# Spreading the softmax reciprocals of each pair's first head by a transpose instead of a product with the identity

## The chip, the cores and the metric

The kernel runs on one core of one Trainium2 chip. A core has five engines that run side by side, each through its own list of instructions: TensorE (PE, matrix products; its weight loads are shown apart as PEld), VectorE (DVE), ScalarE (ACT), GpSimd (POOL) and SyncE (SP), which issues DMA transfers. Products read SBUF and write PSUM, a memory of 128 partitions in eight banks of 512 4-byte words each. The engines meet through semaphores. The metric is the device time of one execution in microseconds (us).

## The reference

One transformer layer for 128 context tokens and 512 latent tokens, with a model width of 1024. The change touches the attention alone: 16 query heads of 64 channels, 4 key and value heads (4 query heads share one).

```python
def block_attention(q, k, v):
    ...
    def one_block(qblk):
        s = jnp.einsum('bqkgd,btkd->bkgqt', qblk, k).astype(jnp.float32) * scale
        p = jax.nn.softmax(s, axis=-1).astype(v.dtype)
        return jnp.einsum('bkgqt,btkd->bqkgd', p, v)
```

Context queries see the 128 context keys. Latent queries see 128 cached context keys and 512 latent keys, 640 in all. Around it stand a projection of the normalised input, a gated short convolution, output projections, and a feed-forward part with a convolution.

## The kernel before, in words

The 640 tokens are five tiles of 128 rows: tile 0 is the context, tiles 1 to 4 are latent. The kernel first normalises the input and makes keys and values, then runs the attention, then everything else (projections, convolution, feed-forward), which is one long stream of products.

The attention runs from about 70 us to 226 us. For each of the four key and value heads g (loop over `NKV`) there are nine steps: one for the context tile, which takes four query heads in two pairs, and two for each latent tile, each of which takes one pair of query heads. That makes 36 steps, 4 of the context and 32 latent. Each step n has this course:

- `score` (L1063 to L1076, products at L1073): queries times keys. The contraction is over 64 channels only, so the two heads of a pair use two row halves of PE's array (`tile_position=(64 * h, 0)`, 64*128 in the profile).
- the maximum over each row (DVE, L1120 or L1085), the exponential with its row sum (ACT, L1128 or L1092), and the split of the result into two 16-bit halves (ACT L1134 or L1099, DVE or POOL L1139, L1141 or L1101).
- `inv` (DVE, L1147 or L1095): the reciprocals of the row sums, one column of 128 values for each head, in `marks` from column 8 on.
- a transposing DMA (SP, L1145 or L1103) that turns the probabilities, so that keys lie in partitions.
- `pv` (L1157 to L1172), on PE. First it spreads the reciprocals (L1162): for each head, the column of 128 reciprocals is read 64 times over (`broadcast_to((128, 64))`) as the stationary operand, and the 4-byte identity matrix is the moving one. The product is a 64 x 128 block, each row of which holds the 128 reciprocals: head 0 of a pair in partitions 0 to 63, head 1 in partitions 64 to 127, in columns 256 to 511 of the bank that the step's result goes to. Then it multiplies values by probabilities (L1170): 30 products of 16-bit operands for a latent step, 12 for a context step, alternating between the heads. The heads use two column halves of the array (`tile_position=(0, 64 * h)`, 128*64 in the profile).
- after the second pair: ACT copies the spread reciprocals to SBUF (`spread`, L1182), DVE multiplies the result by them (`whole`, L1186), and ACT and DVE write the result as two halves (L1189, L1192).

Between these stand the query projections (L709, whole array, 128*128), the transposes of the queries (L1034, 4-byte, whole array), the copies after them, and two products for gates (L1212, L1223, by the helper at L709).

All these pieces are recorded as `work` items with their dependencies and the buffers they need. The order in which they are issued is written out by hand in the string `PLAN` (L50 to L91), which `follow` (L722) walks through: each entry names an item, the engine that does it, and the buffers it takes. The transfers and POOL's work keep that order, too. PE, DVE and ACT run what is issued to them in this order.

A 4-byte product (type float32, not the rounded float32r of L709 and L1073) is executed as two passes, each with its own weight load, and each pass is one record of the profile. A transpose on PE is a product with the identity as moving operand and the flag `is_transpose` set; on 4-byte data it is one pass.

Of the kernel before, what the change touches and what calls it, by code (L numbers as in the profile page):

```python
# [112 lines left out]
def trunk_layer(ctx, tc, x_prompt, x_sample, cache_k, cache_v, c, c_ctx, w_ada, b_ada, g_pre1, g_post1, g_pre2,  # L113
# [600 lines left out]
    def work(name, eng, do, after=(), rooms=()):  # L714
        works.append(Work(name, eng, do, list(after), list(rooms)))
        return works[-1]
# [30 lines left out]
    with tc.tile_pool(name="att", bufs=1) as at:  # L747
# [45 lines left out]
        def at_bank(room, n=512):  # L793
            return bank_of(room.at[0][1])[:, 0:n]
# [4 lines left out]
        def slot(xs, room):  # L799
            return xs[room.at[0][1]]  # L800
# [99 lines left out]
        for t in range(NT):  # L900
# [30 lines left out]
            h = work(f"k{t} hi", "ACT", k_hi, [tk], [pk])  # L931
# [121 lines left out]
        for n, (g, t, pi) in enumerate(steps):  # L1053
# [103 lines left out]
            def pv(g=g, t=t, pi=pi, pvr=pvr, trs=trs, vc_=vc_, mk=mk):  # L1157
                p = at_bank(pvr)
                for i in range(2) if t == 0 else (pi,):
                    for h in range(2):  # L1160
                        c = 8 + 2 * i + h if t == 0 else 8 + h
                        PE.matmul(p[64 * h:64 * h + 64, 256 + 128 * i:384 + 128 * i], mk[:, c:c + 1].broadcast_to((128, 64)), ident,  # L1162
                                  start=True, stop=True, tile_position=(0, 64 * h), skip_group_check=True)
                ks = ((0, 5),) if t == 0 else tuple((k, k) for k in range(5))
                for i in range(2) if t == 0 else (pi,):
                    for k, s in ks:
                        for m, (w, part) in enumerate(((0, 0), (0, 1), (1, 0))):
                            for h in range(2):
                                src = slot(PT, trs[0])[:, 4 * part + 2 * i + h, :] if t == 0 else slot(PT, trs[h])[:, 5 * part + k, :]
                                PE.matmul(p[64 * h:64 * h + 64, i * 128:i * 128 + 128], VH[:, w, s, vc_], src, start=k == 0 and m == 0,  # L1170
                                          stop=k == ks[-1][0] and m == 2, tile_position=(0, 64 * h), skip_group_check=True)
            pvs.append(work(f"pv{n}", "PE", pv, [x[0] for x in pts[n]] + invs + v_ready, [pvr] + trs))  # L1172
            if pi in (None, 1):
                u = vcol[:, 2 * g + (t > 0):2 * g + (t > 0) + 1]
# [1350 lines left out]
```

## Time and profile before

| | us |
|---|---|
| median of 3 runs | 1074.85 (1074.67 to 1075.89) |
| the profiled execution | 1074.79 |
| its span, first to last instruction | 1073.0 |
| PE busy | 1056.8 (98%), 8216 records |
| weight loads busy | 995.4 (93%) |
| DVE busy | 899.9 (84%) |
| ACT busy | 598.4 (56%) |
| POOL busy | 133.1 (12%) |
| L1162, the changed line | 160 records, 16.0 us busy |
| L1170, the products behind it | 1008 records, 34.3 us busy |

A record of PE is a pass; passes overlap at their ends, since the next one enters the array before the last one has left it, so busy times add up to more than the path. The views give, for a group of instructions, line, engine, operation, the tile written and the tiles read, the part of the array used (rows*columns), shape, type and count. The chain of work that ended last starts from the last instruction and goes back, at each step, to what released it. In the chain in order of time, a row has its start, its length, the engine, tile and line, and a count when rows are merged. A list of waits has the waiting engine, tile and line, whom it waited for, the total in us, how many times, and the longest.

### The profile page before, as it was taken

To read this page: it belongs to the slowest core of one execution; us is meant where nothing else is said; L and a number is where in the kernel's file an instruction comes from. 1 tells how busy PE (TensorE), PEld (TensorE's weight loads), DVE (VectorE), ACT (ScalarE), POOL (GpSimd) and SP (SyncE) were. 2 spreads that over 40 slices of the span, in tenths; PEclk is the share of its full clock that TensorE was granted. 3 is DMA by queue.
4 is the path that set the end of the run, shared out by engine and by line. 5 is a ranking of instruction groups with operands and counts; after the bars stand their busy time and mean duration, and the time that the engine had idled before them with its cause. 6 is when DMAs were issued, how large, how long until landed. Compare 5 with 4: busy or idle time off the path is not lost.

```text
span 1073.0 us, 20652 instructions
## 1 busy us (share of the span) xinstructions
PE 1056.8 (98%) x8216; PEld 995.4 (93%) x8216; DVE 899.9 (84%) x1379; ACT 598.4 (56%) x1057; POOL 133.1 (12%) x162
## 2 busy tenths in 40 slices
PE   8999999999999999999999999999999999999997
PEld 6788898899999999999998789999999999999996
DVE  5699999865498999896599678889999988989897
ACT  5478999942344544445322366645555555546673
POOL 1087676500000000000000020000000000000001
PEclk9999999999999999999999999999999999999999
DMA  9829999962244333223668634434544534436873
GB/s 320 256 82 175 190 168 187 191 147 60 75 123 124 93 103 94 79 79 99 189 188 253 198 131 129 121 116 136 166 131 152 150 122 131 152 116 219 277 275 115
DMA packets 243197, 164.02 MB, mean 153 GB/s; under 512 B 94874, under 2 KB 216214, under 8 KB 243102
## 3 DMA queue, kind: packets, MB, share of 16 engines
q1 hardware_dynamic: 242990, 162.68, 55.5%
q8 instruction: 64, 1.05, 0.4%
q14 instruction: 31, 0.25, 0.1%
q10 hardware_dynamic: 112, 0.04, 0.0%
HBM read 123.31 MB, written 17.36 MB: 131 GB/s over the span
## 4 chain that ended last, share of the span: by engine, by line
PE 90%; DVE 3%; ACT 2%; DMA 1%; POOL 1%; issue 1%; SPq 1%; DVEq 0%; ACTq 0%; POOLq 0%
PE b L1274 47%; PE b L235 10%; PE b L237 10%; PE b L236 9%; PE s L709 4%; PE s L1073 2%; PE s L1170 2%; PE s L235 1%; PE s L237 1%; PE s L1162 1%; PE s L478 1%; DVE marks L1120 1%; PE s L236 1%; PE b L1900 1%; ACT P L1134 1%
## 5 line engine op out<-in xcount | busy, mean ns | idle before, releaser
L1274 PE MATMUL b<-ZBr,whi 128*128 128x320 f32 x688 | 152.1, 309 | 0.0
L1274 PE MATMUL b<-MT,whi 128*128 128x320 f32 x608 | 134.4, 309 | 0.0
L1274 PEld LDWEIGHTS b<-ZBr,whi 128*128 128x128 f32 x688 | 114.9, 188 | 0.1
L1274 PE MATMUL b<-ZBr,wlo 128*128 128x320 f32 x344 | 106.1, 308 | 0.0
L1274 PEld LDWEIGHTS b<-MT,whi 128*128 128x128 f32 x608 | 101.7, 188 | 0.0
L1274 PE MATMUL b<-MT,wlo 128*128 128x320 f32 x304 | 94.0, 309 | 0.0
L1261 ACT ACTIVATE whi<-SUM 128x1024 fp32r<-128x1024 f32 x40 | 42.2, 1055 | 78.3 <-DVE SUM L1813 75.7
L1843 DVE SCALAR_TENSOR_TENSOR Y<-C,cffn,Y 128x642 f32<-128x642 f32 x88 | 77.9, 886 | 0.9
L1261 ACT ACTIVATE whi<-WB 128x1024 fp32r<-128x1024 f32 x38 | 40.2, 1058 | 55.5 <-DVE WB L1368 55.5
L1274 PE MATMUL b<-ZBT,whi 128*128 128x320 f32 x320 | 71.0, 308 | 0.0
L1274 PE MATMUL b<-UL,whi 128*128 128x320 f32 x228 | 70.8, 311 | 0.0
L1274 PE MATMUL b<-UH,wlo 128*128 128x320 f32 x228 | 70.1, 307 | 0.0
L1274 PE MATMUL b<-UH,whi 128*128 128x320 f32 x228 | 69.7, 306 | 0.0
L1282 ACT ACTIVATE p<-b 128x320 f32<-128x320 f32 x78 | 34.1, 437 | 55.3 <-PE b L1274 53.5
L1274 PEld LDWEIGHTS b<-ZBr,wlo 128*128 128x128 f32 x344 | 64.6, 188 | 0.0
L1265 DVE TENSOR_TENSOR wlo<-raw,whi 128x1024 fp32r<-128x1024 f32 (+1 forms) x51 | 50.4, 1020 | 13.4 <-ACT whi L1261 13.4
L1274 PEld LDWEIGHTS b<-MT,wlo 128*128 128x128 f32 x304 | 57.1, 188 | 0.0
L1274 PEld LDWEIGHTS b<-ZBT,whi 128*128 128x128 f32 x320 | 54.2, 188 | 1.6
L1120 DVE TENSOR_REDUCE marks<-s 128x1 f32<-128x640 f32 x64 | 52.1, 817 | 4.0 <-PE s L1073 3.8
L1265 DVE TENSOR_TENSOR wlo<-WB,whi 128x1024 fp32r<-128x1024 f32 x38 | 46.5, 1224 | 8.8 <-ACT whi L1261 8.7
L2355 POOL TENSOR_TENSOR ssqs<-ssqs 128x1 f32<-128x1 f32 x4 | 1.4, 356 | 412.9 <-ACT GJ L2349 412.9
L1261 ACT ACTIVATE whi<-raw 128x1024 fp32r<-128x1024 f32 (+1 forms) x51 | 43.5, 892 | 15.4 <-DMA raw<-in_w_o_dram 12.5
(477 smaller groups left out, 3348.1 us busy)
## 6 DMA issues: line engine op xcount, KB each, us to landing
raw<-in_w_in_dram SPq DMA_DIRECT2D x48, 512.0 KB
RAW<-in_w_up_dram SPq DMA_DIRECT2D x40, 512.0 KB
raw<-in_w_down_dram SPq DMA_DIRECT2D x22, 512.0 KB
GA<-in_w_ada_dram SPq DMA_DIRECT2D x16, 512.0 KB
actd<-Y SPq DMA_DIRECT2D x18, 321.0 KB
actl<-ACTb SPq DMA_DIRECT2D x18, 321.0 KB
A<-actl SPq DMA_DIRECT2D x9, 642.0 KB
A<-actd SPq DMA_DIRECT2D x9, 642.0 KB
```

The source lines that it names most:

```text
L235: PE.matmul(out, ah, bh, start=start, stop=False)
L236: PE.matmul(out, ah, bl, start=False, stop=False)
L237: PE.matmul(out, al, bh, start=False, stop=stop)
L709: PE.matmul(out, a, b, start=start and n == 0, stop=stop and n == 2, skip_group_check=True)
L1073: PE.matmul(o[h], q_of(hl, i, rows), kk[kx][rows, g, ks], start=m == 0, stop=m == 2, tile_position=(64 * h, 0), skip_group_check=True)
L1120: V.tensor_reduce(out=mk[:, h:h + 1], in_=s_of(), axis=AX.X, op=ALU.max, negate=True)
L1170: PE.matmul(p[64 * h:64 * h + 64, i * 128:i * 128 + 128], VH[:, w, s, vc_], src, start=k == 0 and m == 0, stop=k == ks[-1][0] and m == 2, ...
L1261: S.activation(to[0], raw, AF.Copy)
L1265: V.tensor_tensor(out=lo, in0=raw, in1=hi.bitcast(F32), op=ALU.subtract)
L1274: PE.matmul(out, p[:, ws], q[:, k, :], start=start and k == 0 and n == 0, stop=stop and k == 3 and n == 2, skip_group_check=True)
L1282: S.activation(t, pair[j][b], AF.Copy)
L1843: V.scalar_tensor_tensor(out=y, in0=crows(j)[i][:, d:d + NACT], scalar=cffn[:, 44 * d + o:44 * d + o + 1], in1=y, op0=ALU.mult, op1=ALU.add)
```

## The change

One argument is added to one call. In each pair the first head's block (h = 0, partitions 0 to 63) is written by a transpose of the broadcast column, with the identity as moving operand as before; the second head's block (h = 1) is still a product. The numbers written are the same reciprocals.

```diff
@@ pv @@
                     for h in range(2):
                         c = 8 + 2 * i + h if t == 0 else 8 + h
                         PE.matmul(p[64 * h:64 * h + 64, 256 + 128 * i:384 + 128 * i], mk[:, c:c + 1].broadcast_to((128, 64)), ident,
-                                  start=True, stop=True, tile_position=(0, 64 * h), skip_group_check=True)
+                                  start=True, stop=True, is_transpose=h == 0, tile_position=(0, 64 * h), skip_group_check=True)
```

## The prediction

> **What bounds the kernel now.** I read the page's table of engines and the chain that ended last, then the busy time of TensorE (PE) in two stretches, then who PE waits for, and last the chain piece by piece through the attention stage, where the changed line runs.
>
> ```profile
> span 1073.0 us, 20652 instructions
> PE 1056.8 (98%) x8216; PEld 995.4 (93%) x8216; DVE 899.9 (84%) x1379; ACT 598.4 (56%) x1057; POOL 133.1 (12%) x162
> PE 90%; DVE 3%; ACT 2%; DMA 1%; POOL 1%; issue 1%; SPq 1%; DVEq 0%; ACTq 0%; POOLq 0%
> ```
>
> ```profile
> core 0: us, PE busy (x), PEclk, DMA share, GB/s
> 75.00:226.00 151.00, 146.56 (x2099) 1.00 1.06 179
> 226.00:1073.00 847.00, 839.95 (x5491) 1.00 0.45 142
> ```
>
> The kernel is bound by PE nearly everywhere: 90% of the chain is PE, and after 226 us no wait of PE on another engine is listed at all. So whatever PE loses or gains in the attention stage (75 to 226 us) is carried to the end unchanged. Only the few waits inside that stage can take something back:
>
> ```profile
> PE s L1034 <- POOL QF L892: 1.8, 2, 1.1
> PE s L1073 <- DVE P L1141: 0.8, 2, 0.6
> PE s L1162 <- DVE QT L1038: 0.5, 1, 0.5
> PE s L1170 <- DMA PT<-P: 0.4, 1, 0.4
> PE s L1162 <- DVE QF L850: 0.4, 1, 0.4
> ```
>
> **The operation.** In each of the 36 steps the two heads' reciprocal sums are spread over 64 partitions each, head 0 into partitions 0 to 63 of a bank, head 1 into 64 to 127.
>
> ```profile
> L1162 PE MATMUL s<-ident,marks x160: 272/273/323, 83.2 to 224.7; 128*64 128x128 f32 x160
> L1034 PE MATMUL s<-ident,QF x40: 271/273/331, 69.1 to 199.8; 128*128 128x128 f32 x40
> ```
>
> A step for latent rows (32 of them) has one product for each head; a step for context rows (4) has two. That makes 32 x 2 + 4 x 4 = 80 products, recorded as 160: a 4-byte product runs as two passes. "128*64" says that it uses half of the array's columns, and that the array stands split in two column halves, as it does for the L1170 products that follow. A 4-byte transpose (L1034: 20 tiles of two transposes, 40 records) is one pass, and uses the array whole (128*128). The middle duration of a pass is 273 ns in both rows, but passes overlap; what one adds to the chain is read from start to start:
>
> ```profile
> 90.86 0.44 PE s L1034 x2
> 91.30 0.37 PE s L1162 x4
> 91.66 0.84 PE s L1170 x30
> 97.80 0.37 PE s L1162 x4
> 102.90 0.22 PE s L1162 x4
> 103.96 0.37 PE s L1034 x2
> 123.01 0.40 PE s L1034 x2
> 159.19 0.22 PE s L1034 x2
> 160.49 0.59 PE s L1162 x8
> ```
>
> Three things are seen here. (a) Two transposes that follow work on the whole array take 0.22 us (159.19), so one takes 0.11 us. (b) Four passes of L1162 that follow L1170 take 0.22 us too (102.90): the two halves work side by side, each through two passes of 0.11 us. (c) Where the work before used the array in another division, the same four passes take 0.37 us (97.80 after row-divided scores, 91.30 after whole-array transposes), and the same two transposes 0.37 us (103.96, after L1170) or 0.40 us (123.01, after scores). A change of division costs 0.15 us: the passes in flight must end, and the first weights can't be loaded ahead.
>
> **The change part by part.** One instruction in each pair gets the transpose flag; nothing is moved, no wait, DMA or other engine's instruction is added. The first head's product still waits for the reciprocals (VectorE, L1147 or L1095), and queued behind it are the same products as before.
>
> Removed: one pass of two for each first head, 40 records of PE (8216 to 8176). Its worth on the path is nothing: by (b) the second head's two passes fill the 0.22 us anyway.
>
> Added: what a transpose does to the division. The trace has no transpose of a 64-wide source, and none beside a product in the other half, so its price has two ends. One end: it runs in its column half, beside the second head; then a pair takes 0.22 us as now, cost 0. A gain is excluded on that path, since the second head's passes are untouched. The other end: it takes the whole array, as L1034 does; then each pair first leaves the column halves, does one transpose alone, and goes back. The nearest row is L1034, the same operation on the same type with the same identity as its moving operand, so I take the second end. By (a) and (c), for each kind of work ahead of the pair:
> - after L1170: before 0.22; after 0.15 + 0.11 for the transpose, and 0.37 for the second head's passes after a whole-array transpose (91.30): 0.63. Adds 0.41.
> - after scores (L1073): before 0.37; after 0.26 + 0.37 = 0.63. Adds 0.26.
> - after whole-array work (L709, L1034): before 0.37; after 0.11 + 0.37 = 0.48. Adds 0.11.
> - the four context steps have two pairs in a row: before 0.59 (160.49); after scores 2 x 0.63 = 1.26, adds 0.67; after whole-array work 0.48 + 0.63 = 1.11, adds 0.52.
>
> How often each occurs is counted in the timeline; the first and the last step behind L1170 and behind L1073:
>
> ```profile
> 101.89 1.01 PE L1170 MATMUL s<-PT,VV 128*64 128x128 f16 x30
> 102.73 0.39 PE L1162 MATMUL s<-ident,marks 128*64 128x128 f32 x4
> ...
> 224.00 0.73 PE L1170 MATMUL s<-PT,VV 128*64 128x128 f16 x20
> 224.56 0.39 PE L1162 MATMUL s<-ident,marks 128*64 128x128 f32 x4
> ```
>
> ```profile
> 97.49 0.31 PE L1073 MATMUL s<-KH,QT 64*128 64x320 f32 x2
> 97.72 0.44 PE L1162 MATMUL s<-ident,marks 128*64 128x128 f32 x4
> ...
> 215.43 0.41 PE L1073 MATMUL s<-KH,QT 64*128 64x320 f32 x2
> 215.76 0.44 PE L1162 MATMUL s<-ident,marks 128*64 128x128 f32 x4
> ```
>
> Latent steps: 13 behind L1170, 13 behind L1073, 6 behind whole-array work; context steps: 2 and 2. Sum: 13 x 0.41 + 13 x 0.26 + 6 x 0.11 + 2 x 0.67 + 2 x 0.52 = 5.33 + 3.38 + 0.66 + 1.34 + 1.04 = 11.75 us more of PE.
>
> The Trainium skill has both halves of this: TensorEngine Tiling (Array Packing), Restrictions and Gotchas, Gotcha 2, says that column tiling and the transpose of 4-byte data exclude each other on trn2, and its Key Properties say that a change of tiling mode, though not of the tile, drains the engine. The second agrees with the 0.37 against 0.22 us above; the first no run here shows yet. By that rule the sum is the 11.75 us, by an independent column half it would be zero.
>
> **What the stage takes back.** Where PE waits for others, and a changed step lies between the place where that other chain left PE and the wait, the wait shrinks by as much:
>
> ```profile
> 78.07 0.44 POOL QF L892
> ...
> 171.67 0.84 DVE marks L1120
> ...
> 191.25 0.44 PE s L1162 x4
> ...
> 198.81 0.84 DVE marks L1120
> ...
> 200.64 1.38 PE s L1073 x12
> ...
> 203.24 0.90 ACT E L1128 x2
> ...
> 225.36 1.03 PE s L1170 x30
> ```
>
> - From 78.07 the chain is on POOL until PE's longest wait (1.1 us, ends 90.86). The context step at 83.22 lies in it: 0.52 hidden.
> - 171.67 to 191.25 is on VectorE and ScalarE; four changed steps (0.26 + 0.41 + 0.26 + 0.11) lie in it, the wait for QF is 0.4: 0.4 hidden, then PE is late itself.
> - 198.81 to 200.64: the context step at 198.70 adds 0.67, the wait for P is 0.6: 0.6 hidden.
> - 203.24 to 225.36 ends in the transfer of the last P tile: 2.3 us are added, the wait is 0.4: 0.4 hidden.
> - The waits for QT (0.5 us), marks and AL have no changed step between them and the place where their chains leave PE: nothing hidden; they move as a whole.
>
> Net: 11.75 - 1.9 = 9.85 us. The profiled execution took 1074.79 us (span 1073.0 and 1.8 around it), 0.06 under the median of 1074.85. 1074.79 + 9.85 = 1084.6 us, +0.9%. If none of the waits gave anything back it would be 1086.5; if part of a change were hidden and it cost 0.10 instead of 0.15, each added change would cost 0.05 less: two behind L1170, one behind scores, three or two in a context step, so 13 x 0.10 + 13 x 0.05 + 2 x 0.15 + 2 x 0.10 = 2.5 us less, 1082.1.
>
> **The rivals.**
> - The transpose runs in its half beside the second head, and the change does nothing for time. For it: L1162's passes do run side by side in 0.22 us. Against it: no transpose in the trace uses half an array. 1074.8 us.
> - The transpose takes the whole array, but next to it nothing has to be emptied, since it comes in the same stream: each pair grows by one pass, 40 x 0.11 = 4.4 us, of which the waits hide some 0.7: 1078.5 us. Against it: rows 103.96 and 91.30, which show the cost in both directions between just these two kinds of work.
> - Faster: the passes of a pair are taken strictly in the order of the program (head 0 first, head 0 second, head 1 first, head 1 second). Then only the middle two overlap, a pair needs three pass times, and to drop head 0's second pass saves one: 40 x 0.11 = 4.4 us, 1070.4 us. It decides only if a pair now takes 0.33 us behind L1170; the row at 102.90 has 0.22, so the second head does not wait for the first one's second pass. The Trainium skill states that order: TensorE: Matmul & The Clock Gate, Part 3, What overlaps and what doesn't, has matmuls strictly in order in start and in end. The trace disagrees with it for the two halves (0.22, not 0.33 us).
>
> **How the numbers follow.** The whole-array transpose with both changes of division: 0.78, 1084.6 us, own range 1081 to 1088. Whole array without emptying: 0.09. No effect: 0.09. Faster by order: 0.04. Slower by over 0.2% (2.1 us, about what separates a change from none here) is 0.78 + 0.09 = 0.87, within 0.09, faster 0.04. The range 1078 to 1088 takes in the first two cases and leaves out the other two, and the tails of the first.
>
> **What the new profile would show.** PE with 8176 records; L1162 in two kinds, 40 single passes and 80 passes of the second heads, the 40 marked 128*128 or followed by a gap; in the chain, some 0.6 us of L1162 between two L1170 blocks in place of 0.22; the attention stage longer by about 10 us and everything behind 226 us shifted and otherwise equal; PE's waits for QF, P and the last transfer gone or shorter. L1162 at 0.22 us behind L1170 would show the first rival, 0.33 the second. I am wrong, too, if PE's delays push the transposing DMAs of P into something else on their queue, or if more than 1.9 us of the waits can be used up.

## The result, and the profile after

The changed kernel took 1084.63 us (median of 4 runs, 1084.31 to 1085.14), the kernel before, beside it on the same chip, 1075.20 (4 runs, 1074.67 to 1075.89). The ratio is 1.0083, with a 95% interval of 1.0070 to 1.0095: slower, by an amount that the prediction (1084.6) had. The sum inside it was not right in every term, and two errors cancelled, so the closeness of the total is luck. This section shows where the time came from; the experiments then test the reasons.

The page's table of engines and its chain, of the kernel after:

```profile
span 1083.4 us, 20572 instructions
PE 1067.3 (99%) x8176; PEld 999.5 (92%) x8176; DVE 901.8 (83%) x1379; ACT 600.4 (55%) x1057; POOL 132.6 (12%) x162
PE 93%; DVE 3%; DMA 2%; POOL 1%; ACT 1%; issue 0%; DVEq 0%; SPq 0%; POOLq 0%; ACTq 0%
```

PE has the 8176 records that were forecast, 40 fewer, and yet 10.5 us more of busy time. The profiled execution took 1085.14 us, 0.5 over the median.

Two stretches of it, the attention stage and the rest, with the busy time of each engine and PE's clock:

```profile
core 0: us, PE busy (x) PEld busy (x) DVE busy (x) ACT busy (x) POOL busy (x), PEclk, DMA share, GB/s
75.00:236.50 161.50, 157.73 (x2073) 137.39 (x2072) 135.79 (x292) 136.54 (x313) 93.93 (x88) 1.00 0.97 168
236.50:1083.40 846.90, 839.82 (x5486) 805.05 (x5480) 713.97 (x955) 421.90 (x659) 16.25 (x36) 1.00 0.45 142
```

The rest takes 846.90 us with 839.82 of PE, against 847.00 and 839.95 before: it is only moved back. The clock is 1.00 in both stretches, so the throttle has no part in it. From here on "the stage" is the time between the start of four query transposes near 75 us and the first product at L235, both rows of the chain in order of time. Before:

```profile
74.96 0.53 PE s L1034 x4
...
228.37 0.38 PE b L235
```

That is 153.41 us. The same chain after:

```profile
75.94 0.53 PE s L1034 x4
98.77 0.41 PE s L1162 x2
99.34 0.85 PE s L1170 x26
103.47 0.85 PE s L1170 x26
104.32 0.41 PE s L1162 x2
104.90 0.85 PE s L1170 x26
122.94 0.29 PE s L1162 x2
123.40 0.85 PE s L1170 x26
165.94 0.99 PE s L1162 x5
167.46 1.62 PE s L709 x12
238.78 0.39 PE b L235
```

The stage now takes 162.84 us, 9.43 more. (The 0.98 us by which it starts later lie ahead of the changed code, where the chain waits for the first loads.)

**What one step costs.** The order of the instructions is unchanged on every engine, so the counts of the prediction (13 latent steps behind L1170, 13 behind scores, 6 behind whole-array work, 4 context steps) hold, and only the prices are to be read. Behind L1170 a pair and its products took 0.22 + 0.84 = 1.06 us (102.90 to 103.96 before). Now one block of products starts at 103.47, the next at 104.90: 1.43 us, 0.37 more. Behind scores it was 0.37 + 0.84 = 1.21 and is 1.42 (98.77 to the end of the row at 99.34): 0.21 more. Behind whole-array work it was 1.21 and is 1.31 (122.94 to the end of the row at 123.40): 0.10 more. A context step behind scores took 0.59 us and 0.34 for its products (160.49 to 161.42 before) and now takes 1.52 (165.94 to 167.46): 0.59 more. One behind whole-array work (123.41 to 124.33 before, 126.07 to 127.57 after) takes 0.58 more. It gains nothing from standing there, since its first weight load waits for ScalarE's L872 in both kernels (0.17 and 0.16 us); the other one, at 84 us inside PE's wait for POOL, is taken at the same price.

The sum is 13 x 0.37 + 13 x 0.21 + 6 x 0.10 + 2 x 0.59 + 2 x 0.58 = 10.5 us, where 11.75 were forecast.

**Why a step may be a little cheaper than forecast.** PE's timeline between two blocks of products, after (the merged row of L1162 holds the transpose, from 104.25, and the second head's first pass, from 104.48):

```profile
103.99 0.33 PE L1170 MATMUL s<-PT,VV 128*64 128x128 f16 x3
104.25 0.55 PE L1162 MATMUL s<-ident,marks 128*64 128x128 f32 x2
104.49 0.35 PE L1170 MATMUL s<-PT,VV 128*64 128x128 f16 x3
104.64 0.27 PE L1162 MATMUL s<-ident,marks 128*64 128x128 f32 x1
```

Between the starts of the second head's two passes stand products of L1170, which come behind both in the program. The view does not name the head, but they can be head 0's, in the other column half, whose spread is done. So the second head's second pass is partly beside useful work; what that is worth no run measures. The transposes are recorded as 128*64, like everything else on this line; the form doesn't show that they use the array whole. The starts do: 0.23 us lie between the transpose and the other head's first pass, where two halves that run side by side start 0.01 us apart (in t_short, below).

**PE's waits in the stage**, after (who waited for whom: total us, times, longest):

```profile
PE s L1034 <- POOL QF L892: 1.3, 2, 0.7
PE s L1034 <- DVE marks L1147: 0.7, 1, 0.7
PE s L1162 <- DVE QF L850: 0.5, 1, 0.5
PE s L1162 <- DVE QT L1038: 0.5, 1, 0.5
PE s L1034 <- DVE AL L1192: 0.3, 1, 0.3
PE s L1162 <- DVE marks L1123: 0.2, 1, 0.2
PE s L1073 <- DVE P L1141: 0.2, 1, 0.2
```

The wait for QF from POOL fell from 1.8 to 1.3, that for P from 0.8 to 0.2, that for the last transfer (0.4) is gone, all three as forecast. But the wait for QF of L850 did not shrink (0.4 to 0.5), and a wait of 0.7 for L1147 is new. The whole list was 4.3 us before (the five rows shown and two of 0.2 each) and is 3.7 now: it gave back 0.6 us, not 1.9. 10.5 - 0.6 = 9.9 against the 9.43 measured; the remaining 0.5 us is left over, and where it lies was not found.

**The new wait** has a cause that I had not thought of. VectorE and POOL around the place, first before, then after (the chain leaves PE there at the fourth context step's maxima):

```profile
183.26 0.17 DVE L1086 TENSOR_SCALAR marks<-marks 128x4 f32<-128x4 f32 x1
183.40 1.41 POOL L1139 TENSOR_TENSOR P<-E,P 128x640 f16<-128x640 f32 x1 [2.17 <-ACT P L1134]
```

```profile
190.47 1.35 DVE L1086 TENSOR_SCALAR marks<-marks 128x4 f32<-128x4 f32 x1
190.39 1.41 POOL L1139 TENSOR_TENSOR P<-E,P 128x640 f16<-128x640 f32 x1 [2.54 <-ACT P L1134]
```

Adding a constant to four values per partition took 1.35 us instead of 0.17. Before, it started 0.14 us ahead of a POOL product; now it starts 0.08 us behind it, and it ends at 191.82, POOL's product at 191.80. The last experiment below tests whether the one holds the other.

### The profile page after: what moved, and what is told of

Read it like the earlier page. It is cut to its first block, busy times and chain, and to the rows that moved or that the text cites. A ratio compares the mean times of both kernels' runs of the same rounds, so it can differ in the third digit from the quotient of the medians.

```text
span 1083.4 us, 20572 instructions
## 1 busy us (share of the span) xinstructions
PE 1067.3 (99%) x8176; PEld 999.5 (92%) x8176; DVE 901.8 (83%) x1379; ACT 600.4 (55%) x1057; POOL 132.6 (12%) x162
## 4 chain that ended last, share of the span: by engine, by line
PE 93%; DVE 3%; DMA 2%; POOL 1%; ACT 1%; issue 0%; DVEq 0%; SPq 0%; POOLq 0%; ACTq 0%
PE b L1274 47%; PE b L235 10%; PE b L237 9%; PE b L236 9%; PE s L709 5%; PE s L1073 3%; PE s L1170 3%; PE s L1162 2%; DMA araw<-in_w_ada_dram 1%; DMA XT<-in_w_ada_dram 1%; PE s L235 1%; PE s L237 1%; PE s L478 1%; PE b L1900 1%; PE s L236 1%; POOL wlo L831 0%
```

## Experiments: is it the transpose, or the division of the array?

My theory is that a 4-byte transpose takes the array whole, so that a pair leaves the column halves and comes back, at a price per change of division. The rivals are that each transpose empties the array by itself, and that the flag costs something wherever it stands.

**t_twice: each transpose issued twice.**

```diff
-                    for h in range(2):
+                    for h in (0, 0, 1):
```

> Every first head's transpose is issued twice in a row, to the same place; all else as in the changed kernel (1084.6 us). Theory (the time goes into changes of the array's division, and a transpose next to another one is one pass of 0.11 us): 40 x 0.11 = 4.4 us more, 1089.0 us. Rival (each 4-byte transpose empties the array by itself, whatever stands beside it): a second one costs 0.26 like the first one behind scores, 40 x 0.26 = 10.4 us more, 1095 us. Rival (the second one runs beside something and is free): 1084.6 us.

1088.91 us, ratio to before 1.013 (1.0113 to 1.0147). From its chain in order of time:

```profile
98.94 0.52 PE s L1162 x3
104.71 0.52 PE s L1162 x3
```

0.52 where the changed kernel has 0.41, behind scores (98.94) and behind L1170 (104.71) alike: the second transpose costs 0.11 us, one pass. The stage (75.98 to 242.52) is 3.7 us longer than after (40 x 0.11 = 4.4; PE's waits are 3.5 us instead of 3.7, and the other 0.5 us is left open). A transpose that stands behind another transpose is cheap, so the price of the change is not in the transposes themselves; the rival that each one empties the array falls.

**t_last: the second head first, the transpose behind it.**

```diff
-                    for h in range(2):
+                    for h in (1, 0):
```

> Same operations as the changed kernel, the second head's product issued ahead of the first head's transpose in each pair. Theory (each change of division costs 0.15 us): one change more in the 13 steps behind scores, two more in the 6 behind whole-array work, one or two more in the four context steps, none more behind L1170: 13 x 0.15 + 6 x 0.30 + 2 x 0.15 + 2 x 0.30 = 4.7 us over the changed kernel, 1089.3 us. Rival (the transpose has one price wherever it stands): 1084.6 us.

1086.84 us, ratio 1.0113 (1.0098 to 1.0128). Its chain behind scores, behind L1170, and behind whole-array work:

```profile
98.11 0.59 PE s L1162 x3
...
103.91 0.45 PE s L1162 x3
104.36 0.96 PE s L1170 x30
...
122.74 0.59 PE s L1162 x3
```

With the products (0.96 in all three places) it comes to 1.55, 1.41 and 1.55 us, against 1.42, 1.43 and 1.31 after. Behind L1170 there are two changes of division in either order, and the price is the same within 0.02. Behind scores the transpose in the middle needs a change more (0.13), behind whole-array work two more (0.24). So one change costs 0.12 to 0.13 us here, where I had reckoned with 0.15. The stage (75.02 to 240.44) is 2.6 us longer than after, less than the 4.7 expected: the prices give 13 x 0.13 + 6 x 0.24 + 4 x 0.13 - 13 x 0.02 = 3.4 for latent and context steps (a context step reads 1.64 us where it was 1.50 or 1.52). PE's waits are 3.3 us instead of 3.7, and the other 0.4 us is left open. The same instructions in another order cost different amounts, as the count of changes says, and a cost of the flag alone would not.

**t_short: 2-byte transposes in the column half.** From the kernel before.

```diff
+        ident16 = at.tile([128, 128], F16, name="ident16")
+        V.tensor_copy(ident16, ident)
...
+                        if h == 0:
+                            for q in range(2):
+                                PE.matmul(p.bitcast(F16)[0:64, 512 + 256 * i + 128 * q:640 + 256 * i + 128 * q],
+                                          mk.bitcast(F16)[:, 2 * c + 1:2 * c + 2].broadcast_to((128, 64)), ident16,
+                                          start=True, stop=True, is_transpose=True, tile_position=(0, 0), skip_group_check=True)
+                            continue
```

> The first head's transpose is made of 2-byte elements: two transposes of the column's upper halves with a 2-byte identity fill the same 64 x 128 words (so the words are not the reciprocals, and the attention's values are others; VectorE makes the 2-byte identity once). Both stay in the column half. Theory (what costs is that a 4-byte transpose takes the whole array): no change of division, the second head's two passes fill 0.22 us as in the kernel before: 1075.2 us, within 0.5. Rival (any transpose takes the whole array or empties it): two passes and the same changes as in the changed kernel, 1084.6 to 1089 us.

1075.01 us, ratio 1.0003 (0.9994 to 1.0013): no difference from before. PE's timeline behind scores (L1166 is the transposes, L1170 here the second head's product, L1178 the products of values):

```profile
102.14 0.24 PE L1166 MATMUL s<-ident,marks 128*64 128x128 f16 x1
102.15 0.32 PE L1170 MATMUL s<-ident,marks 128*64 128x128 f32 x1
102.22 0.22 PE L1166 MATMUL s<-ident,marks 128*64 128x128 f16 x1
102.28 0.22 PE L1178 MATMUL s<-PT,VV 128*64 128x128 f16 x1
```

A 2-byte transpose starts 0.01 us ahead of the other half's 4-byte product and runs beside it. So the flag costs nothing, nor does a transpose in half the array. What costs is the transpose of four-byte data.

**p_whole: no transpose, but head 0's product over the whole array.** From the kernel before; the second head's block then overwrites partitions 64 to 127.

```diff
-                        PE.matmul(p[64 * h:64 * h + 64, 256 + 128 * i:384 + 128 * i], mk[:, c:c + 1].broadcast_to((128, 64)), ident,
+                        m = 64 if h else 128
+                        PE.matmul(p[64 * h:64 * h + m, 256 + 128 * i:384 + 128 * i], mk[:, c:c + 1].broadcast_to((128, m)), ident,
```

> No transpose: the first head's reciprocals are spread by a product over all 128 partitions, on the whole array, and the second head's product then overwrites partitions 64 to 127 as before. Theory (the division is what costs, not the transpose): the same changes of division as in the changed kernel and two passes where it has one, 40 x 0.11 = 4.4 us over it: 1089.0 us. Rival (the transpose flag is what costs): no flag, so only the passes that no longer overlap, 40 x 0.22 = 8.8 us over the kernel before at most and 40 x 0.11 = 4.4 us at least, 1079.6 to 1084 us.

1091.28 us, ratio 1.0152 (1.0137 to 1.0167). Its chain (L1163 is the spread, L1171 the products) behind scores, L1170's counterpart and whole-array work:

```profile
98.05 0.60 PE s L1163 x3
103.98 0.60 PE s L1163 x3
123.38 0.40 PE s L1163 x3
```

There is no transpose in this kernel, and leaving the halves costs as much and more: 0.60 where after has 0.41. Behind whole-array work, where no change precedes it, it is 0.40 to 0.29, the 0.11 of the one pass more. Behind a change it is 0.19 more, 0.08 beyond the pass, which I had not expected. The 0.08 us lies in the first pass: behind scores its weight load, of 128 columns, takes 0.18 us and starts together with it (both at 97.98), and the pass is 0.38 us long; the transpose after has a load of 64 columns, 0.11 us, and a pass of 0.30 (both from 98.70). A load that isn't hidden would explain it; no run tests that. By these rows the steps are some 7 us longer than after; the stage (75.09 to 244.13) is 6.2 longer, where 4.4 were expected. PE's waits take 0.3 of the difference, and 0.5 us is left open. The rival that the cost comes with the flag falls here for good: a whole-array step between column halves is enough.

**h_second and h_first: the transpose in some pairs only.**

```diff
-                                  start=True, stop=True, is_transpose=h == 0, tile_position=(0, 64 * h), skip_group_check=True)
+                                  start=True, stop=True, is_transpose=h == 0 and pi == 1, tile_position=(0, 64 * h), skip_group_check=True)
```

The lines are those of the changed kernel. h_first has `pi != 1` in place of `pi == 1`, so that the two share out the 40 pairs, 16 and 24.

> The transpose in the second pair of each latent tile only (16 of the 40), products elsewhere. By the chain of the changed kernel a step grows by 0.37 us behind L1170, by 0.21 behind scores, by 0.10 behind whole-array work. Theory (the price goes by what stands ahead): most of these 16 stand right behind the first pair's L1170, 13 x 0.37 + 3 x 0.2 = 5.4 us, less what the last transfer's wait of 0.4 us hides: 5.0 us over the kernel before, 1079.8 us. Rival (one price for every transpose, 9.4 us / 40 = 0.24): 16 x 0.24 = 3.8 us, 1078.5 us.

> The transpose in the first pairs and the context steps only (24 of the 40). Theory: the rest of the sum, 10.5 - 5.4 = 5.1 us less what the other waits hide (up to 1): 4.1 to 5.1 us over the kernel before, about 1079.3 us, and no more than h_second. Rival (one price): 24 x 0.24 = 5.6 us, 1080.3 us, well over h_second.

h_second took 1079.63 us, ratio 1.0044 (1.0030 to 1.0057), with a stage (74.91 to 233.21) 4.89 us longer than before; h_first 1081.29, ratio 1.0058 (1.0043 to 1.0072), with 5.98 (74.88 to 234.27). The expectation that the second pairs cost more rested on a wrong count of what stands ahead of them. In the written order 8 of the 16 stand behind L1170, 3 behind scores and 5 behind whole-array work; the other 24 pairs are 16 first pairs of latent tiles, of which 5, 10 and 1 stand behind these, and the 4 context steps with two pairs each. With the prices above: 8 x 0.37 + 3 x 0.21 + 5 x 0.10 = 4.1 us, and 5 x 0.37 + 10 x 0.21 + 0.10 + 2 x 0.59 + 2 x 0.58 = 6.4. The intervals are too wide to tell these from one price for every pair, which had h_first slower than h_second too. That the price goes by what stands ahead rests on the rows of the chain and on t_last, not on these two times. That h_second came out at the time expected (1079.8) is luck: a smaller sum of prices, and new waits on top. h_first missed (1079.3, and no more than h_second).

The two stages together are 1.4 us more than the whole change (10.87 to 9.43). The waits account for it, and for a little more. A wait for L1147 is in both, 1.0 us in h_second and 0.8 in h_first, and in h_second the wait for P is whole again (0.8 us):

```profile
PE s L1034 <- DVE marks L1147: 1.0, 1, 1.0
```

All of PE's waits in the stage are 5.4 us in h_second and 4.4 in h_first, against 4.3 before and 3.7 after. So half of the change already brings the new wait in full, and gives back less of the old ones. Price and waits together are 4.1 + 1.1 = 5.2 (measured 4.89) and 6.4 + 0.1 = 6.5 (measured 5.98).

## Experiments: could the reciprocals be spread with fewer changes of division?

If passes and changes are what costs, then one transpose per pair, of a tile in which the columns are already repeated 64 times, spreads both heads at once. Five kernels made such a tile on another engine. None beat the kernel before.

**w_front and w_end: VectorE writes the reciprocals 64 times over.** w_front puts the one whole-array transpose where the spread was; w_end puts both pairs' transposes behind the second pair's products, so that the stage changes division for them only once in two steps.

```diff
+                invs = [work(f"inv{n}", "DVE", lambda mk=mk, wd=wds[n]: V.reciprocal(wd[0], mk[:, 4:6].unsqueeze(2).broadcast_to((128, 2, 64))), exs)]
...
-                    for h in range(2):
-                        c = 8 + 2 * i + h if t == 0 else 8 + h
-                        PE.matmul(p[64 * h:64 * h + 64, 256 + 128 * i:384 + 128 * i], mk[:, c:c + 1].broadcast_to((128, 64)), ident,
-                                  start=True, stop=True, tile_position=(0, 64 * h), skip_group_check=True)
+                    x = wds[n][i if t == 0 else 0]
+                    PE.transpose(p[:, 256 + 128 * i:384 + 128 * i], x.rearrange("p h c -> p (h c)"), ident)
```

> Both heads of a pair by one 4-byte transpose over the whole array, ahead of the values' products: VectorE writes the two reciprocal columns 64 times over into a 128-wide tile (in the room of two tables that are no longer read), and no product with the identity is left. Theory (changes of division at the prices seen: 0.15 in, 0.15 out, 0.11 a pass): behind L1170 two changes and a pass for 0.22 before, about 0.14 to 0.19 more, 13 times; behind scores about as before, 13 times; behind whole-array work 0.11 to 0.13 less, 6 times; context steps 0.1 to 0.2 less, 4 times. Sum +0.2 to +1.8 us on the kernel before: 1075 to 1077 us. Rival (what cost in the changed kernel was the second head's two passes left alone, not the changes): with them gone it is faster than before by the passes, 40 x 0.11 = 4.4 us, 1070.4 us.

> As w_front, but the transposes of both pairs of a tile stand behind the values' products of the second pair, where PE mostly goes back to the whole array anyway. Theory: the products' own 0.22 us are gone in 40 pairs (8.8 us less), 40 passes of 0.11 come back (4.4 us more), and a change of division is added only where scores follow (9 places, at most 0.15 each, 1.35 us): 3 us less than the kernel before, 1071.7 us; if the entry into L1170 is cheaper without a product ahead, down to 1070. Rival (the copies of the spread reciprocals, which wait for the transposes, and the longer reciprocals on VectorE hold up the chain): no gain, 1074 to 1076 us.

1093.86 us (ratio 1.0176, 1.0162 to 1.0190) and 1094.38 (1.0178, 1.0165 to 1.0192). Both expectations missed by far, for one reason, seen in the groups of the kernel before and of w_front (the last columns are busy us and mean ns, then idle time ahead and its releaser):

```profile
L1147 DVE RECIPROCAL marks<-marks 128x2 f32<-128x2 f32 x32 | 4.9, 157 | 2.0 <-ACT s L1128 2.0
```

```profile
L1157 DVE RECIPROCAL tabk<-marks 128x128 f32<-128x128 f32 x22 | 20.6, 939 | 1.6 <-ACT s L1138 1.6
```

A reciprocal of 128 values per partition takes 0.94 us, one of two 0.157: about 6 ns for each value more. 32 such in latent steps and 8 in context steps are some 32 us of new work (40 x 0.94, less the 36 narrow ones at 0.16) on VectorE, which then is busy for 158 of the 165 us between 75 and 240 us of w_end and takes the place of PE as the bound. What PE would have saved can't be read from these two.

**c_front, c_end and c_pool: the narrow reciprocal, and a copy that repeats it.** c_front and c_end are w_front and w_end, but with a copy by VectorE; c_pool is c_end with the copy on POOL.

```diff
+                    V.reciprocal(mk[:, 8:10], mk[:, 4:6])
+                    V.tensor_copy(wd[0], mk[:, 8:10].unsqueeze(2).broadcast_to((128, 2, 64)))
...
```

> As w_front, but the reciprocals are taken of two values for each step again (0.157 us) and then copied 64 times over on VectorE (an estimate of 0.2 us each, 40 of them, 8 us of VectorE in a stage where it is busy some 87%). Theory (changes of division as priced): PE 0.2 to 1.8 us over the kernel before, of VectorE's 8 us up to a third on the path: 1075 to 1079 us. Rival (the wide operations of VectorE are the bound whatever their length): stays near 1093 us.

> As w_end with the narrow reciprocal and the copy on VectorE. Theory: PE 3 us under the kernel before, VectorE's copies give back up to a third of 8 us: 1072 to 1074.5 us. Where the transposes stand decides: 2 to 4 us under c_front. Rival (the division doesn't matter once the second head's product is gone): equal to c_front.

> As c_end with the copies on POOL (an estimate of 0.4 us each by POOL's 0.83 us for 256 columns, 16 us in all, POOL being busy some 62% of the stage). Theory: 1072 us if POOL's copies lie in its waits; up to 1077 us where they hold up the split of the probabilities (L1139) behind them.

1082.37 us (ratio 1.0065, 1.0043 to 1.0087), 1083.89 (1.0077, 1.0054 to 1.0100) and 1077.52 (1.0025, 1.0015 to 1.0034). All missed, c_pool by the least (it was to take 1077 at most). The copies of c_front (count, then shortest, median and longest in ns), one of them beside POOL, and a wait of c_end:

```profile
L1160 DVE COPY tabk<-marks x22: 226/228/1466, 84.5 to 229.2; 128x128 f32<-128x128 f32 x22
```

```profile
119.01 1.41 POOL L1150 TENSOR_TENSOR P<-E,P 128x640 f16<-128x640 f32 x1 [1.08 <-ACT P L1145]
119.08 1.43 DVE L1160 COPY tabk<-marks 128x128 f32<-128x128 f32 x1
```

```profile
PE s L1080 <- DVE P L1152: 3.9, 5, 2.5
```

Alone, a copy takes 0.23 us, about the 0.2 that I had set down. But 11 of the 32 copies of latent steps in c_front took longer. Each of these started while POOL had a product of 256 or more values per partition running, and ended 0.08 to 0.09 us behind it; together they took some 5.3 us more than 0.23 each. Two that started during POOL's L879, which has four values per partition and took 1.02 us, took 0.23. The next section comes back to this. The probabilities P, which VectorE also makes, come late (3.9 us of PE's waits in c_end, where it was 0.8); how much of that is the copies' own time, how much the holding, was not separated. c_end was to be 2 to 4 us under c_front and is not, but with VectorE late on both sides this says nothing on where the transposes should stand.

On POOL the copies delay QF instead: 2.7 us of waits for 1.8. In c_pool PE has 1998 records and 147.52 us busy in its stage (75.26 to 229.25), against 2119 and 148.97 in the stage before, so the passes were in fact saved, but other engines' lateness takes the gain back, and the stage is 0.6 us longer than before. Whether fewer changes of division would pay with a free engine is left open; none is free here.

## Experiment: is the new wait VectorE held by POOL?

**v_columns: the changed kernel, with the shift of the maxima done column by column.**

```diff
-                    V.tensor_scalar(out=mk[:, 0:4], in0=mk[:, 0:4], scalar1=SHIFT * math.log(2), scalar2=None, op0=ALU.add)
+                    for j in range(4):
+                        V.tensor_scalar(out=mk[:, j:j + 1], in0=mk[:, j:j + 1], scalar1=SHIFT * math.log(2), scalar2=None, op0=ALU.add)
```

> The changed kernel with one edit on VectorE: the shift of the four maxima in a context step (L1086) is done in four instructions of one value instead of one of four. In the changed kernel one of the four L1086 took 1.35 us, from 190.47 to 191.82; a GpSimd product (L1139) ran from 190.39 to 191.80. Theory A: the instruction of four values was held until the GpSimd product ended, and that 1.2 us is why the wait for QF at the end of this chain stayed 0.5 us and why a new wait of 0.7 us (for L1147) came. Shifts of one value (L1123) take 0.14 to 0.16 us in all 32 cases, 12 of them during a product of L1139, so in this kernel none of the 16 shifts is over 0.2 us, the wait for L1147 is gone, that for QF is at most 0.1 us longer or shorter or gone, and the time is 0.7 to 1.2 us under the changed kernel: 1083.4 to 1083.9, a ratio of about 1.0078. Theory B: VectorE waited there for something else than the form of this instruction; then the first of the four shifts or the next instruction is as long, the wait for L1147 stays at 0.7 us, and the time stays at 1084.6 us, a ratio of about 1.0087.

1082.87 us, ratio to before 1.0077 (1.0063 to 1.0091). That is 1.8 us under the median after; the kernel before, run beside it, was 0.6 us faster as well. VectorE and POOL at the place, and the ends of the stage:

```profile
189.48 0.34 DVE L1087 TENSOR_SCALAR marks<-marks 128x1 f32<-128x1 f32 x4
189.41 1.41 POOL L1140 TENSOR_TENSOR P<-E,P 128x640 f16<-128x640 f32 x1 [2.54 <-ACT P L1135]
```

```profile
75.16 0.53 PE s L1034 x4
236.78 0.38 PE b L235
```

The shift again starts 0.07 us behind POOL's product, and is done in 0.34 us for all four columns, in the middle of that product. PE's wait for the reciprocals is gone from the list, which is now 2.7 us in all, and the stage is 161.62 us, 1.22 shorter than after: the whole of the 1.2 us by which the one instruction had been longer. Theory A holds for the instruction and for the new wait; the intervals of the two ratios overlap, so it rests on the traces, not on the times. The same hold is in other places. In the kernel before, the shift of the second context step started at 108.33 inside a product that POOL had begun at 107.45; it took 0.55 us, to 108.88, POOL's product ended at 108.86, and the changed kernel has the same 0.55 us at 110.11. In t_last, h_second and h_first the fourth shift took 1.35 to 1.37 us, again inside a POOL product, and the 11 copies of c_front ended with POOL's products in the same way.

The Trainium skill has the mechanism: SBUF — State Buffer, SBUF: two separate sides, calls the port pair that VectorE shares with GpSimd "an exclusive lock, not a bandwidth split", taken for a whole instruction by whichever starts first, where the VectorE operation runs in a mode that uses two ports or has two SBUF inputs. The trace agrees on the length: 1.35 us, ending within 0.02 us of POOL's product. In which mode the shift runs, no view shows; what the runs show is that one value at a time isn't held. The two copies of c_front beside L879 weren't held either, which a hold for the whole of any POOL instruction would not explain.

Theory A was wrong in one part: the wait for QF (L850) is 0.4 us in v_columns too, as before. It does not come from the hold. In the kernel before, two paths lead to it, the one over VectorE and ScalarE and one from PE's query transposes, and they meet in a copy of ScalarE:

```profile
187.28 0.38 PE L1034 MATMUL s<-ident,QF 128*128 128x128 f32 x2
187.70 0.39 ACT L1036 ACTIVATE QT<-s 128x256 fp32r<-128x256 f32 x1
```

The copy starts only 0.04 us behind the end of the transposes that it reads (187.66). From there to the end of the wait it is 3.6 us before (187.66 to 191.25) and in v_columns (194.04 to 197.61). The four changed steps stand ahead of the transposes, so they push its start and PE's arrival at the wait back alike.

## Why the prediction was right, and which terms were not

- **The removed pass is worth nothing on the path: not contradicted.** PE lost 40 records and no chain got shorter by them, but no run removes the pass alone; it rests on the 0.22 us at 102.90 in the kernel before.
- **The transpose takes the array whole: right**, though the sign that I gave for it (128*128 in the records) does not appear. It is shown by what the two-byte kind does in the half (ratio 1.0003) and by p_whole, which pays without a transpose. The first rival (beside the second head, 1074.8) falls by this. By the Trainium skill, TensorEngine Tiling (Array Packing), Restrictions and Gotchas, Gotcha 2, column tiling and a 4-byte transpose exclude each other. The trace now agrees: 1.43 us for 1.06 behind L1170.
- **Each change of division costs: right, but mis-sized.** The term of 0.15 us is 0.12 to 0.13 by t_last. Behind L1170 a step came to 0.37 where 0.41 was forecast, behind scores 0.21 (0.26), behind whole-array work 0.10 (0.11), context steps 0.59 and 0.58 (0.67 and 0.52). The sum of the steps is 10.5 us, 1.25 under the 11.75 of the prediction. It had also overlooked that products start ahead of head 1's last pass; how much of the 1.25 that is was not separated. The second rival (no emptying, 40 x 0.11) would add 0.11 behind L1170; it falls by the 0.37 that was added, and by t_twice, in which a transpose that needs no emptying costs just the 0.11.
- **The waits give back 1.9 us: three of the four places right, the fourth wrong.** QF from POOL 0.5, P 0.6 and the last transfer 0.4 came as forecast. The step "171.67 to 191.25 is on VectorE and ScalarE ... 0.4 hidden" failed: a second path to that wait starts on PE, at the query transposes behind the four changed steps, and is as long within 0.05 us, so nothing hides there, with the hold (0.5 us) or without it (0.4 in v_columns). Besides, the shifted work put a VectorE instruction 0.08 us behind a POOL product that it had been 0.14 us ahead of, which made a new wait of 0.7 us. So all waits together gave back 0.6. Without the hold (v_columns) they give back 1.6, which is near the forecast but not by its terms: QF from POOL 0.4, P 0.6, the last transfer 0.4, and 0.2 for AL, where nothing was forecast.
- **The total** of +9.85 against the 9.43 of the stage is near by luck: prices 1.25 too high, hidden time 1.3 too high, and 0.5 us that these readings leave over. With the hold taken away the stage is 8.2 us longer than before, which is about the price of the change itself.
- **The third rival** (strict order of the program, faster) had already been against the trace of before; the changed kernel's products that run ahead of the other half's pass say the same.
- **Everything behind the stage only moves: right** (846.90 against 847.00 us).

## What to carry to other kernels

Count changes of the array's division in the order in which work stands, and price them from start to start in the chain; don't count a pass less in a half whose other half is busy as a gain unless a row shows it, and remember that a whole-array pass between two column-half blocks cost 0.37 us here. Before counting a stall as a place where added time hides, look at what else runs in that stretch: a shift of 0.2 us between VectorE and POOL cost 1.2 us, and a second path to the same wait left nothing to hide. And before moving a spread of columns to another engine, price it there by its number of values and see what POOL runs beside it, since engines that were off the path became the bound.

## What the runs showed that I had not expected

- Products start ahead of a pass that comes earlier in the program (104.49 against 104.64), which two column halves that work separately would allow.
- Two-byte transposes in one column half run beside a 4-byte product in the other at no cost (1.0003).
- The first 128-wide 4-byte pair of passes behind a change took some 0.08 us more than a transpose and the one extra pass explain (0.60 against 0.41 + 0.11). Its weight load took 0.18 us instead of 0.11; whether that is the cause was not tested.
- A VectorE instruction of four values per partition was held for 1.2 us by a POOL product. The shift of one value (L1123) ran 12 times of 32 during such a product in the changed kernel and never took more than 0.16 us. In v_columns three of the four groups of four such shifts ran beside a POOL product, and each group took 0.34 us, like the one that ran alone.
- A VectorE copy of 128 values per partition takes 0.23 us, and up to 1.47 us when it starts inside a POOL product.
- A VectorE reciprocal costs 0.157 us for two values per partition and 0.94 us for 128.
